# Sample attention of a decode step: its products on VectorE, its loads on GpSimd's queue, key halves on neighbouring partitions

## The chip, the cores and the metric

The kernel runs on one core of one Trainium2 chip. A core has five engines with a queue of instructions each, which run in order: TensorE (PE, with its weight loads shown as PEld), VectorE (DVE), ScalarE (ACT), GpSimd (POOL) and SyncE (SP). Any of SP, ACT and POOL can issue DMA transfers; 16 DMA engines carry them out. Engines wait for each other on semaphores. The metric is the device time of one execution in microseconds.

## The reference

One layer of a hybrid decoder, for a prompt of 1024 tokens and for 8 sequences of 4 new tokens (the sample). Both go through the same projections; the change concerns the attention of the sample's 32 tokens over their cached keys and values. For each of three head groups (window and dilation 128/1, 512/4, 2048/16), with 4 heads of 64 columns:

```python
def _dilated_sample(q, k_all, v_all, slopes, window, dil, L):
    j = jnp.arange(window // dil + 1)
    idx = L + jnp.arange(T)[:, None] - j[None, :] * dil
    valid = idx >= 0
    kg, vg = k_all[:, jnp.maximum(idx, 0)], v_all[:, jnp.maximum(idx, 0)]
    s = jnp.einsum('bthd,btjhd->bhtj', q, kg) * (1.0 / math.sqrt(Dh))
    s = jnp.where(valid, s - slopes * (j * dil), NEG_INF)
    m = jnp.max(s, axis=-1, keepdims=True)
    p = jnp.exp(s - m); l = jnp.sum(p, axis=-1, keepdims=True)
    o = jnp.einsum('bhtj,btjhd->bthd', p / l, vg)
    lse = m + jnp.log(l)
```

The three groups' outputs are combined with weights softmax(lse), projected, gated together with a convolution branch, and added to x; a feed-forward layer, a small per-layer gate and a norm follow. Everything is float32.

## The kernel before, in words

Activations lie transposed, 1056 tokens (1024 of the prompt, 32 of the sample) in three chunks of 352 columns. Each large product is done as three matmuls on float32r parts: a weight slab is loaded by SP (tile wst, L93), ACT rounds it to whi (L103), DVE takes the rest as wlo (L104), and PE runs L120, L121 and L122 into a PSUM tile mm. A tile of eight K-blocks takes 24 matmuls.

The order of stages is: input norm and small projection; convolution projections and gates; then, for two pairs of heads and in each for three groups, the projections q, k, v (copied out of PSUM by ACT at L651), the prompt's scores (L824 on PE into ps_s, and a mask, add and row maximum on DVE, L829), the transposed values (L851), and the sample's tokens, which PE transposes (L859) and SP writes to a small DRAM buffer scr (L862). At the end of a pair comes the prompt's softmax: maxima through PE (L683 to L711), exponentials on ACT (L745), transposes of the scores (L747), copies to pt by ACT (L751) or, for half of the parts of pair 0, DVE (L753), products with the values (L724), and normalisation (L775 to L791). After pair 1 the convolution branch is projected: L886 loads a gate into et (two buffers), 12 matmuls make a tile, DVE multiplies it into et (L891), L892 stores it. Attention output, mixing projection, feed-forward and output follow, without sample attention.

The tiles mm and ps_s have two buffers each in this part, so PE goes on to the tile after next only when the reader of the first has finished.

Sample attention has no matmuls. It is a list of small steps, queued in `bg` by `sample_ops` and taken from there by `pump` between the projections; the Tile scheduler then gives every engine's queue its final order by a simulated timeline. A pair has 2 heads x 32 tokens = 64 rows. The 128 cached keys of a row are cut into two halves of 64: half 0 lies on partitions 0 to 63, half 1 (with the new keys) on partitions 64 to 127. Per pair and group:

- `load` (L546): POOL clears the unused end of the bias tile (L549), SP loads the bias (L552, one DMA for each half) and the query (sq, L555, twice, from scr).
- `k_part`, for eight tiles kt of 8 keys x 64 columns and a tile of new keys: SP loads kt (L584, one DMA for each half, 64 partitions x 2 KB; new keys L595 or L598), POOL multiplies it by the query (L558), DVE sums over the 64 columns (L559).
- `smax`: bias, maximum, exponential (L563 to L566).
- `v_part`, for eight tiles of values and one of new values: POOL multiplies (the first straight into vacc, L571, the others in place, L573) and DVE adds to vacc (L574); at the end DVE sums vacc into oacc (L606).

kt has four buffers, so a load waits until the tile four before it has been summed or added. At the end of a pair `sample_out` combines the groups and the two halves: maxima are exchanged through PE (L612 to L619), and a matmul with `both`, a sum of two identity halves, adds row p and row p + 64 (L630).

Of the kernel before, what the change touches and what calls it, by code (L numbers as in the profile page):

```python
# [13 lines left out]
OP = mybir.AluOpType  # L14
# [15 lines left out]
NEG = -1e30  # L30
DIL = (1, 4, 16)
NB = (8, 8, 8)
SOFF = (0, 132, 261, 390)
# [14 lines left out]
def hybrid_layer(ctx: ExitStack, tc: tile.TileContext, I, O):  # L48
    nc = tc.nc
    te, ve, ac, gp, sy = nc.tensor, nc.vector, nc.scalar, nc.gpsimd, nc.sync  # L50
# [12 lines left out]
    ident = consts.tile([128, 128], F32, name="ident")  # L63
# [240 lines left out]
    scr = [[dram.tile([3, 32, 128], F32, name=f"scr{i}{g}") for g in range(3)] for i in range(2)]  # L304
# [224 lines left out]
    CK, HK = 8, 64  # L529
    oacc = sp.tile([128, 3, 64], F32, name="oacc")  # L530
    sv = sp.tile([128, 8, 3], F32, name="sv")
    vacc = sp.tile([128, CK, 64], F32, name="vacc")
    both = sp.tile([128, 64], F32, name="both")
    ve.tensor_tensor(both, ident[:, :64], ident[:, 64:], op=OP.add)

    def rows(t, width, first, pair, n):

        return bass.AP(tensor=t.tensor, offset=t.offset + 2 * pair * width + first,
                       ap=[[4 * width, 32], [width, 2], [1, n]])

    def sample_ops(pair, g):
        n_new = 4 if g == 0 else 1
        nk = HK + n_new
        st = {}

        def load():  # L546
            st["s"] = sp.tile([128, HK + 4], F32, name="sc", tag="sc", bufs=2)
            st["b"] = b = sp.tile([128, HK + 4], F32, name="sbias", tag="sbias", bufs=2)
            gp.memset(b[0:64, HK:], NEG)  # L549
            for hf in range(2):  # L550
                n = nk if hf else HK
                sy.dma_start(b[64 * hf:64 * hf + 64, :n], rows(I["sbias"], SOFF[3], SOFF[g] + HK * hf, pair, n))  # L552
            st["q"] = a = sp.tile([128, 64], F32, name="sq", tag="sq", bufs=2)
            for hf in range(2):
                sy.dma_start(a[64 * hf:64 * hf + 64], scr[pair][g][0].rearrange("t (e d) -> (t e) d", d=64))  # L555

        def k_part(kt, off, n):
            gp.tensor_tensor(kt, kt, st["q"][:, None, :].to_broadcast([128, n, 64]), op=OP.mult)  # L558
            ve.tensor_reduce(st["s"][:, off:off + n], kt, axis=AX, op=OP.add)  # L559

        def smax():
            s = st["s"][:, :nk]
            ve.tensor_tensor(s, s, st["b"][:, :nk], op=OP.add)  # L563
            ve.tensor_reduce(sv[:, 0, g:g + 1], s, axis=AX, op=OP.max)
            ve.tensor_scalar(sv[:, 1, g:g + 1], sv[:, 0, g:g + 1], -1.0, None, op0=OP.mult)
            ac.activation(s, s, AF.Exp, bias=sv[:, 1, g:g + 1], accum_out=sv[:, 2, g:g + 1])  # L566

        def v_part(vt, off, n):
            p = st["s"][:, off:off + n, None].to_broadcast([128, n, 64])
            if off == 0:  # L570
                gp.tensor_tensor(vacc, vt, p, op=OP.mult)  # L571
            else:
                gp.tensor_tensor(vt, vt, p, op=OP.mult)  # L573
                ve.tensor_tensor(vacc[:, :n], vacc[:, :n], vt, op=OP.add)  # L574

        def kt_tile():
            return sp.tile([128, CK, 64], F32, name="kt", tag="kt", bufs=4)

        def steps(nm, part):
            for i in range(0, HK, CK):  # L580
                def f(i=i):
                    kt = kt_tile()
                    for hf in range(2):
                        sy.dma_start(kt[64 * hf:64 * hf + 64].rearrange("p n d -> p (n d)"),  # L584
                                     rows(I[f"{nm}g{g}"], 128 * 64, (HK * hf + i) * 64, pair, CK * 64))
                    part(kt, i, CK)
                bg.append(f)

            def new():
                kt = kt_tile()  # L590
                src = scr[pair][g]["qkv".index(nm)]
                gp.memset(kt[0:64, :n_new], 0.0)
                if g == 0:
                    for j in range(4):
                        sy.dma_start(kt[64 + 16 * j:80 + 16 * j, :4],  # L595
                                     src.rearrange("(n b) (e d) -> (b e) n d", n=4, d=64))
                else:
                    sy.dma_start(kt[64:, 0], src.rearrange("t (e d) -> (t e) d", d=64))  # L598
                part(kt[:, :n_new], HK, n_new)
            bg.append(new)  # L600

        bg.append(load)
        steps("k", k_part)
        bg.append(smax)
        steps("v", v_part)
        bg.append(lambda: ve.tensor_reduce(oacc[:, g], vacc.rearrange("p n d -> p d n"), axis=AX, op=OP.add))  # L606

    def sample_out(pair):

        ve.tensor_reduce(sv[:, 3, 0:1], sv[:, 0], axis=AX, op=OP.max)  # L610
        ps = misc()
        te.transpose(ps[0:1, :128], sv[:, 3, 0:1], ident)  # L612
        room = sp.tile([128, CK, 64], F32, name="kt", tag="kt", bufs=4)
        row, ow = room[0:1, 0:2], room[:, 2:4].rearrange("p a b -> p (a b)")[:, :65]
        o, so = room[0:64, 4], room[:, 5, :32]
        ve.tensor_copy(row.rearrange("o h t -> o (h t)"), ps[0:1, :128])
        ve.tensor_tensor(row[:, 0], row[:, 0], row[:, 1], op=OP.max)
        ve.tensor_copy(row[:, 1], row[:, 0])
        te.transpose(ps[:, 128:129], row.rearrange("o h t -> o (h t)"), ident[0:1, 0:1])  # L619
        ve.tensor_scalar(sv[:, 3, 1:2], ps[:, 128:129], -1.0, None, op0=OP.mult)  # L620
        ac.activation(sv[:, 4], sv[:, 0], AF.Exp, bias=sv[:, 3, 1:2])
        ve.tensor_tensor(sv[:, 5], sv[:, 4], sv[:, 2], op=OP.mult)
        ve.tensor_reduce(ow[:, 64:65], sv[:, 5], axis=AX, op=OP.add)
        ve.tensor_scalar(ow[:, :64], oacc[:, 0], sv[:, 4, 0:1], None, op0=OP.mult)
        for g in (1, 2):
            ve.scalar_tensor_tensor(ow[:, :64], oacc[:, g], sv[:, 4, g:g + 1], ow[:, :64],
                                    op0=OP.mult, op1=OP.add)

        ps = misc()
        te.matmul(ps[:64, :65], both, ow, start=True, stop=True)  # L630
        ve.reciprocal(sv[:64, 6, 0:1], ps[:64, 64:65])
        ve.tensor_scalar(o, ps[:64, :64], sv[:64, 6, 0:1], None, op0=OP.mult)
        ps = misc()
        te.transpose(ps[:64, :64], o, ident[:64, :64])
        for e in range(2):
            ve.tensor_copy(so[64 * e:64 * e + 64], ps[:64, :64].rearrange("d (t e) -> d e t", e=2)[:, e])
        split(ohi[:, pair, TP:], olo[:, pair, TP:], so)
# [160 lines left out]
    for pair in range(2):  # L798
        S, VT = [], []
        mcol = ap_.tile([128, 3, 8, 2], F32, name="mcol", tag="mcol", bufs=2)  # L800
        for g in range(3):
# [4 lines left out]
            for i, nm in enumerate("qkv"):  # L806
                t = ap_.tile([128, T], F32, name=nm, tag=nm, bufs=1)
# [3 lines left out]
                if i == 1:  # L811

                    q, k = qkv
# [3 lines left out]
                    for b0 in range(0, 8, 2):  # L817

                        pss2 = [pss.tile([128, 2, 256], F32, name="ps_s", tag="ps_s") for e in range(2)]
                        for b in (b0, b0 + 1):  # L820
                            q0, k0, nk, _ = BL[g][b]
                            for e in range(2):
                                h = slice(64 * e, 64 * e + 64)
# [512 lines left out]
```

## Time and profile before

| | |
|---|---|
| time of the runs | 1683.91 us median of 3 (1677.45 to 1688.59) |
| the profiled execution | 1681.99 us, of which 1680.2 us are its span |
| granted TensorE clock in it | 0.988 |
| PE, DVE, ACT, POOL busy | 1619.0, 1038.5, 579.1, 200.0 us |
| DMA | 233.81 MB, mean 139 GB/s |

A page of the profile gives each engine's busy time and, in 40 slices of 42 us, its busy share in tenths. Rows of groups read: line, engine, operation, output <- input, shapes, count | busy us, mean ns of one | idle time of the engine just before, and what ended it. Rows of waits read: engine, line and tile that waited <- what ended the wait: us in total, times, longest. Rows of the timeline read: start, duration, engine, line, operation, with the idle time before it in brackets. "SPq" is the issue of a DMA on SP's queue; busy time of POOL does not contain DMA issues.

### The profile page before, as it was taken

To read this page: it belongs to the slowest core of one execution; us is meant where nothing else is said; L and a number is where in the kernel's file an instruction comes from. 1 tells how busy PE (TensorE), PEld (TensorE's weight loads), DVE (VectorE), ACT (ScalarE), POOL (GpSimd) and SP (SyncE) were. 2 spreads that over 40 slices of the span, in tenths; PEclk is the share of its full clock that TensorE was granted. 3 is DMA by queue.
4 is the path that set the end of the run, shared out by engine and by line. 5 is a ranking of instruction groups with operands and counts; after the bars stand their busy time and mean duration, and the time that the engine had idled before them with its cause. 6 is when DMAs were issued, how large, how long until landed. Compare 5 with 4: busy or idle time off the path is not lost.

```text
span 1680.2 us, 27443 instructions
## 1 busy us (share of the span) xinstructions
PE 1619.0 (96%) x11091; PEld 1584.8 (94%) x11091; DVE 1038.5 (62%) x1791; ACT 579.1 (34%) x1064; POOL 200.0 (12%) x178
## 2 busy tenths in 40 slices
PE   8999999999989988989999999999999999999996
PEld 7999999988889888989999999999999999999996
DVE  7799996125453656475776666676665533437666
ACT  7211223422253325342344333333333321215542
POOL 3100000005550543250000000000000000000003
PEclk9999999999999999999999999999999999999998
DMA  8535554615441457584245444432223422311422
GB/s 306 182 127 177 187 176 151 204 50 158 144 125 34 138 175 221 165 277 160 102 157 200 159 155 161 152 133 77 77 77 118 142 87 85 117 48 57 128 72 108
DMA packets 85487, 233.81 MB, mean 139 GB/s; under 512 B 14576, under 2 KB 32432, under 8 KB 84272
## 3 DMA queue, kind: packets, MB, share of 16 engines
q1 hardware_dynamic: 76272, 174.15, 32.0%
q10 hardware_dynamic: 9088, 57.91, 10.1%
q8 instruction: 87, 1.43, 0.3%
q14 instruction: 40, 0.33, 0.1%
HBM read 187.49 MB, written 88.37 MB: 164 GB/s over the span
## 4 chain that ended last, share of the span: by engine, by line
PE 40%; issue 9%; DVE 7%; DMA 4%; ACT 1%; POOL 0%; SPq 0%; DVEq 0%; ACTq 0%; POOLq 0%
PE mm L203 6%; PE mm L205 6%; PE mm L120 6%; PE mm L204 6%; PE mm L122 6%; PE mm L121 6%; DMA wst<-in_w_fu 2%; DVE wq L145 1%; PE N L724 1%; DVE hlo L209 1%; DVE ws L150 1%; DMA et<-gcd 1%; DVE hq L209 0%; DVE fg L1071 0%; DVE ga L956 0%
## 5 line engine op out<-in xcount | busy, mean ns | idle before, releaser
L120 PE MATMUL mm<-hhi,whi 128*128 128x352 f32 x1424 | 466.7, 328 | 8.4 <-ACT hhi L367 4.4
L121 PE MATMUL mm<-hlo,whi 128*128 128x352 f32 x1424 | 462.7, 325 | 2.0 <-DVE hlo L209 2.0
L122 PE MATMUL mm<-hhi,wlo 128*128 128x352 f32 x1424 | 463.4, 326 | 0.0
L203 PE MATMUL mm<-hq,wq 128*128 128x264 f32 x1232 | 350.7, 285 | 2.3 <-DVE fg L1076 1.9
L204 PE MATMUL mm<-hq,wq 128*128 128x264 f32 x1232 | 350.5, 285 | 2.0 <-DVE hq L209 2.0
L205 PE MATMUL mm<-hq,wq 128*128 128x264 f32 x1232 | 350.3, 285 | 0.0
L120 PEld LDWEIGHTS mm<-hhi,whi 128*128 128x128 f32 x1424 | 269.4, 189 | 14.6 <-ACT hhi L367 4.9
L121 PEld LDWEIGHTS mm<-hlo,whi 128*128 128x128 f32 x1424 | 270.6, 190 | 4.4 <-DVE hlo L209 2.8
L122 PEld LDWEIGHTS mm<-hhi,wlo 128*128 128x128 f32 x1424 | 270.7, 190 | 2.2 <-issue 2.0
L203 PEld LDWEIGHTS mm<-hq,wq 128*128 128x128 f32 x1232 | 232.4, 189 | 3.3 <-ACT fg L1072 2.0
L204 PEld LDWEIGHTS mm<-hq,wq 128*128 128x128 f32 x1232 | 232.6, 189 | 2.4 <-DVE hq L209 2.4
L205 PEld LDWEIGHTS mm<-hq,wq 128*128 128x128 f32 x1232 | 232.1, 189 | 0.0
L103 ACT ACTIVATE whi<-wst 128x1024 fp32r<-128x1024 f32 (+2 forms) x100 | 97.3, 974 | 316.7 <-PE mm L121 303.7
L121 PE MATMUL mm<-mid,whi 128*128 128x352 f32 x528 | 169.5, 323 | 1.6 <-DVE mid L209 1.6
L122 PE MATMUL mm<-mid,wlo 128*128 128x352 f32 x528 | 168.4, 323 | 0.0
L120 PE MATMUL mm<-mid,whi 128*128 128x352 f32 x528 | 167.6, 324 | 0.0
L104 DVE TENSOR_TENSOR wlo<-wst,whi 128x1024 fp32r<-128x1024 f32 (+2 forms) x100 | 115.6, 1157 | 63.5 <-ACT whi L103 62.2
L425 DVE SCALAR_TENSOR_TENSOR acc<-U,vec,acc 128x1024 f32<-128x1024 f32 x120 | 147.1, 1279 | 0.4
L558 POOL TENSOR_TENSOR kt<-kt,sq 128x512 f32<-128x512 f32 (+2 forms) x54 | 68.9, 1300 | 461.4 <-DMA sq<-scr 445.9
L1138 POOL TENSOR_TENSOR y<-x,r 128x704 f32<-128x704 f32 x8 | 15.2, 1944 | 883.4 <-ACT r L938 883.4
L1122 DVE TENSOR_TENSOR x<-mm,x 128x352 f32<-128x352 f32 x96 | 49.4, 523 | 106.5 <-PE mm L122 106.1
L121 PEld LDWEIGHTS mm<-mid,whi 128*128 128x128 f32 x528 | 99.1, 188 | 1.9 <-DVE mid L209 1.9
(214 smaller groups left out, 2129.7 us busy)
## 6 DMA issues: line engine op xcount, KB each, us to landing
o_rest<-in_rest ACTq DMA_DIRECT2D x32, 768.0 KB, 5.3
wst<-in_w_in SPq DMA_DIRECT2D x42, 512.0 KB, 5.3
kt<-in_kg SPq DMA_DIRECT2D x96, 128.0 KB, 2.9
kt<-in_vg SPq DMA_DIRECT2D x96, 128.0 KB, 3.2
midd<-fg ACTq DMA_DIRECT2D x44, 264.0 KB, 3.3
mst<-midd SPq DMA_DIRECT2D x22, 528.0 KB, 4.6
wst<-in_w_fg SPq DMA_DIRECT2D x22, 512.0 KB, 3.9
wst<-in_w_fu SPq DMA_DIRECT2D x22, 512.0 KB, 5.7
```

The source lines that it names most:

```text
L103: last_act[0] = ac.activation(hi[:, :n, :], st[:, :n, :], AF.Copy)
L104: ve.tensor_tensor(lo[:, :n, :], st[:, :n, :], hi[:, :n, :].bitcast(F32), op=OP.subtract)
L120: te.matmul(ps, hi[:, k, :], rh, start=(i == 0), stop=False)
L121: te.matmul(ps, hi[:, k, :], rl, start=False, stop=False)
L122: te.matmul(ps, lo[:, k, :], rh, start=False, stop=(i == n - 1))
L145: ve.tensor_tensor(t[:, 1], x, t[:, 0].bitcast(F32), op=OP.subtract)
L203: te.matmul(ps, w[:, 0, i], h[:, 0, i], start=start and i == 0, stop=False, skip_group_check=True)
L204: te.matmul(ps, w[:, 0, i], h[:, 1, i], start=False, stop=False, skip_group_check=True)
L205: te.matmul(ps, w[:, 1, i], h[:, 0, i], start=False, stop=i == k - 1, skip_group_check=True)
L425: ve.scalar_tensor_tensor(acc[:, ct, :TP], U[:, ct, j:j + TP], vcol(w0 + j), acc[:, ct, :TP], op0=OP.mult, op1=OP.add)
L558: gp.tensor_tensor(kt, kt, st["q"][:, None, :].to_broadcast([128, n, 64]), op=OP.mult)
L1122: ve.tensor_tensor(x1[:, m, cs_(c)], ps[:, :C], x1[:, m, cs_(c)], op=OP.add)
```

## The change

The products of `k_part` and `v_part` are VectorE instructions. Every load of the sample attention is issued from GpSimd's queue. The two halves of a row's keys lie on partitions 2r and 2r + 1 instead of r and r + 64, so that a tile of keys or values is one DMA over 128 partitions (source rows 64 keys apart), and the query one DMA that reads each row twice; bias and new keys go to every second partition. POOL clears the whole bias tile and all rows of the tile of new keys, and the loads then fill the parts that hold data. `both` becomes the sum of the even and the odd columns of the identity, and `sample_out` exchanges maxima between neighbouring columns. Line numbers after the helper are lower by one. The arithmetic is the same.

```diff
-    ve.tensor_tensor(both, ident[:, :64], ident[:, 64:], op=OP.add)
-
-    def rows(t, width, first, pair, n):
-
-        return bass.AP(tensor=t.tensor, offset=t.offset + 2 * pair * width + first,
-                       ap=[[4 * width, 32], [width, 2], [1, n]])
+    ve.tensor_tensor(both, ident[:, 0::2], ident[:, 1::2], op=OP.add)
+
+    def dims(t, offset, ap):
+        return bass.AP(tensor=t.tensor, offset=t.offset + offset, ap=ap)
...
-            gp.memset(b[0:64, HK:], NEG)
+            gp.memset(b, NEG)
             for hf in range(2):
                 n = nk if hf else HK
-                sy.dma_start(b[64 * hf:64 * hf + 64, :n], rows(I["sbias"], SOFF[3], SOFF[g] + HK * hf, pair, n))
+                gp.dma_start(b[hf::2, :n], dims(I["sbias"], 2 * pair * SOFF[3] + SOFF[g] + HK * hf,
+                                                [[4 * SOFF[3], 32], [SOFF[3], 2], [1, n]]))
             st["q"] = a = sp.tile([128, 64], F32, name="sq", tag="sq", bufs=2)
-            for hf in range(2):
-                sy.dma_start(a[64 * hf:64 * hf + 64], scr[pair][g][0].rearrange("t (e d) -> (t e) d", d=64))
+            q = scr[pair][g][0]
+            gp.dma_start(a, dims(q, 0, [[64, 64], [0, 2], [1, 64]]))
 
         def k_part(kt, off, n):
-            gp.tensor_tensor(kt, kt, st["q"][:, None, :].to_broadcast([128, n, 64]), op=OP.mult)
+            ve.tensor_tensor(kt, kt, st["q"][:, None, :].to_broadcast([128, n, 64]), op=OP.mult)
             ve.tensor_reduce(st["s"][:, off:off + n], kt, axis=AX, op=OP.add)
...
             if off == 0:
-                gp.tensor_tensor(vacc, vt, p, op=OP.mult)
+                ve.tensor_tensor(vacc, vt, p, op=OP.mult)
             else:
-                gp.tensor_tensor(vt, vt, p, op=OP.mult)
+                ve.tensor_tensor(vt, vt, p, op=OP.mult)
                 ve.tensor_tensor(vacc[:, :n], vacc[:, :n], vt, op=OP.add)
...
                     kt = kt_tile()
-                    for hf in range(2):
-                        sy.dma_start(kt[64 * hf:64 * hf + 64].rearrange("p n d -> p (n d)"),
-                                     rows(I[f"{nm}g{g}"], 128 * 64, (HK * hf + i) * 64, pair, CK * 64))
+                    gp.dma_start(kt.rearrange("p n d -> p (n d)"),
+                                 dims(I[f"{nm}g{g}"], (2 * pair * 128 + i) * 64,
+                                      [[4 * 128 * 64, 32], [HK * 64, 4], [1, CK * 64]]))
                     part(kt, i, CK)
...
-                gp.memset(kt[0:64, :n_new], 0.0)
+                gp.memset(kt[:, :n_new], 0.0)
                 if g == 0:
                     for j in range(4):
-                        sy.dma_start(kt[64 + 16 * j:80 + 16 * j, :4],
+                        gp.dma_start(kt[32 * j + 1:32 * j + 32:2, :4],
                                      src.rearrange("(n b) (e d) -> (b e) n d", n=4, d=64))
                 else:
-                    sy.dma_start(kt[64:, 0], src.rearrange("t (e d) -> (t e) d", d=64))
+                    gp.dma_start(kt[1::2, 0], src.rearrange("t (e d) -> (t e) d", d=64))
                 part(kt[:, :n_new], HK, n_new)
...
-        row, ow = room[0:1, 0:2], room[:, 2:4].rearrange("p a b -> p (a b)")[:, :65]
+        row, ow = room[0:1, 0:2].rearrange("o a b -> o (a b)").rearrange("o (t h) -> o t h", h=2), room[:, 2:4].rearrange("p a b -> p (a b)")[:, :65]
...
-        ve.tensor_tensor(row[:, 0], row[:, 0], row[:, 1], op=OP.max)
-        ve.tensor_copy(row[:, 1], row[:, 0])
+        ve.tensor_tensor(row[:, :, 0], row[:, :, 0], row[:, :, 1], op=OP.max)
+        ve.tensor_copy(row[:, :, 1], row[:, :, 0])
```

How the change moves instructions on VectorE and on GpSimd's queue stands at the places of the prediction that rest on it, as the build of each kernel lists them: engine queues in order, with the semaphores that an instruction waits for in brackets. DMAHW0 to 7 are transfers issued by SP or ACT, DMASW0 to 7 those issued by POOL; the number 49 is a label of the list.

More of the change, by code (lines that the diff above doesn't have):

```diff
@@ L613, in sample_out @@
         room = sp.tile([128, CK, 64], F32, name="kt", tag="kt", bufs=4)
-        row, ow = room[0:1, 0:2], room[:, 2:4].rearrange("p a b -> p (a b)")[:, :65]
+        row, ow = room[0:1, 0:2].rearrange("o a b -> o (a b)").rearrange("o (t h) -> o t h", h=2), room[:, 2:4].rearrange("p a b -> p (a b)")[:, :65]
         o, so = room[0:64, 4], room[:, 5, :32]
-        ve.tensor_copy(row.rearrange("o h t -> o (h t)"), ps[0:1, :128])
-        ve.tensor_tensor(row[:, 0], row[:, 0], row[:, 1], op=OP.max)
-        ve.tensor_copy(row[:, 1], row[:, 0])
-        te.transpose(ps[:, 128:129], row.rearrange("o h t -> o (h t)"), ident[0:1, 0:1])
+        ve.tensor_copy(row, ps[0:1, :128].rearrange("o (t h) -> o t h", h=2))
+        ve.tensor_tensor(row[:, :, 0], row[:, :, 0], row[:, :, 1], op=OP.max)
+        ve.tensor_copy(row[:, :, 1], row[:, :, 0])
+        te.transpose(ps[:, 128:129], row.rearrange("o t h -> o (t h)"), ident[0:1, 0:1])
         ve.tensor_scalar(sv[:, 3, 1:2], ps[:, 128:129], -1.0, None, op0=OP.mult)
```

## The prediction

> **What bounds the kernel now.** I read the page first, then the stage of the sample attention by windows, then who waited for whom in it, last the stretch around one wait.
>
> ```profile
> span 1680.2 us, 27443 instructions
> PE 1619.0 (96%) x11091; PEld 1584.8 (94%) x11091; DVE 1038.5 (62%) x1791; ACT 579.1 (34%) x1064; POOL 200.0 (12%) x178
> PE   8999999999989988989999999999999999999996
> DVE  7799996125453656475776666676665533437666
> POOL 3100000005550543250000000000000000000003
> ```
>
> PE is busy for 96% of the span, so a change elsewhere can only remove or add PE's gaps. POOL works between about 370 and 700 us, on the lines of this change, and there PE's digits fall to 8 in a few slices. The same stretch in us (columns: PE, PEld, DVE, ACT, POOL busy, granted clock, DMA):
>
> ```profile
> 360.00:410.00 50.00, 47.04 (x281) 42.99 (x281) 24.36 (x52) 13.24 (x22) 23.26 (x21) 1.00 0.41 123
> ...
> sum 400.00, PE 371.11 PEld 344.35 DVE 221.16 ACT 144.46 POOL 163.47; mean PE 46.39 PEld 43.04 DVE 27.65 ACT 18.06 POOL 20.43
> ```
>
> From 360 to 760 us PE is idle for 400 - 371 = 29 us: all that a perfect change here could give, 1.7% of the span. DVE is busy for 221 of the 400. Who keeps PE waiting, and what DVE and POOL wait for (us in total, times, longest):
>
> ```profile
> PE ps_s L824 <- DVE mcol L829: 13.0, 12, 2.4
> PE N L724 <- DVE pt L753: 3.5, 1, 3.5
> PE mm L120 <- DVE et L891: 3.4, 2, 2.1
> PE ps_s L747 <- DVE pt L753: 1.3, 1, 1.3
> ...
> DVE sc L559 <- POOL kt L558: 60.8, 34, 12.1
> DVE vacc L574 <- POOL kt L573: 31.9, 18, 3.8
> ...
> POOL kt L573 <- DMA kt<-in_vg: 20.8, 11, 4.9
> POOL kt L558 <- DMA kt<-in_kg: 13.3, 10, 2.9
> ```
>
> PE waits for DVE: 13.0 us for the masks of the prompt's scores (L829), 4.8 us for the copies of transposed scores (L753), 3.4 us for the conv projection's evacuation (L891). DVE in turn sat 60.8 + 31.9 = 92.7 us waiting for POOL's products, and POOL for the loads of keys and values. One stretch shows the chain:
>
> ```profile
> 396.95 4.58 SPq L584 DMA_DIRECT2D kt<-in_vg  x5
> 401.63 1.94 SPq L595 DMA_DIRECT2D kt<-scr  x4
> ...
> 403.25 4.51 POOL L573 TENSOR_TENSOR kt<-kt,sc 128x512 f32<-128x512 f32 x4 [2.69 <-DMA kt<-in_vg]
> ...
> 404.33 2.96 DVE L574 TENSOR_TENSOR vacc<-vacc,kt 128x512 f32<-128x512 f32 x2 [3.02 <-POOL kt L573]
> 407.22 0.28 DVE L829 CUSTOM_DVE_ANT_0 S<-ps_s,bias 128x128 f32<-128x128 f32 x1
> ...
> 402.64 0.32 PE L120 MATMUL mm<-hhi,whi 128*128 128x352 f32 x1
> 402.80 0.32 PE L121 MATMUL mm<-hlo,whi 128*128 128x352 f32 x1
> 407.90 0.92 PE L824 MATMUL ps_s<-k,q 64*128 64x128 f32 x4 [2.21 <-DVE mcol L829]
> ```
>
> Two adds on DVE wait 3.02 us for POOL, POOL 2.69 us for a load on SP's queue; the mask behind them comes at 407.22 and PE loses 2.21 us. Matmuls start 0.16 us apart, so a tile of 24 covers 3.9 us of such lateness, and a tile of 12 in the conv projection 1.9 us.
>
> **The change part by part.** (1) The products of L558, L571 and L573 go from POOL to DVE. Group 0 of pair 0, value half, on DVE, before (L574 the add, L829 a mask):
>
> ```order
> L829 ISA S_3507,mcol<-ps_s,bias 128x256
> L829 ISA mcol 128x1
> L574 TENSOR_TENSOR vacc<-vacc,kt 128x512 [waits DMAHW0_49,DMAHW6_49,DVE_49,Pool_49]
> L574 TENSOR_TENSOR vacc<-vacc,kt 128x512 [waits DMAHW1_49,DMAHW2_49,DVE_49,Pool_49]
> L829 ISA S_3507,mcol<-ps_s,bias 128x128 [waits PE_49]
> ```
>
> and now, one line number lower (L572 is the product, L573 the add):
>
> ```order
> L828 ISA S_3498,mcol<-ps_s,bias 128x256
> L828 ISA mcol 128x1
> L573 TENSOR_TENSOR vacc<-vacc,kt 128x512 [waits DVE_49]
> L572 TENSOR_TENSOR kt<-kt,sc 128x512 [waits DMASW7_49]
> L573 TENSOR_TENSOR vacc<-vacc,kt 128x512 [waits DVE_49]
> L572 TENSOR_TENSOR kt<-kt,sc 128x512 [waits DMASW0_49]
> L573 TENSOR_TENSOR vacc<-vacc,kt 128x512 [waits DVE_49] x2
> L828 ISA S_3498,mcol<-ps_s,bias 128x128 [waits PE_49]
> ```
>
> Between the same two masks stand now four adds and two products instead of two adds, and DVE itself waits for POOL's loads (DMASW), with the mask and, further on, the weight splits of L104 queued behind. The prices:
>
> ```profile
> L574 DVE TENSOR_TENSOR vacc<-vacc,kt 128x512 f32<-128x512 f32 x42 | 41.8, 995 | 32.9 <-POOL kt L573 31.9
> L559 DVE TENSOR_REDUCE sc<-kt 128x8 f32<-128x512 f32 x48 | 32.7, 684 | 60.8 <-POOL kt L558 60.8
> L104 DVE TENSOR_TENSOR wlo<-wst,whi 128x1024 fp32r<-128x1024 f32 x22 | 30.9, 1405 | 2.1 <-ACT whi L103 1.9
> ...
> L145 DVE TENSOR_TENSOR wq<-ws,wq 128x512 fp32r<-128x512 f32 x76 | 52.1, 685 | 3.6 <-ACT wq L144 3.6
> ...
> L104 DVE TENSOR_TENSOR wlo<-wst,whi 128x1024 fp32r<-128x1024 f32 x21 | 25.7, 1224 | 45.0 <-ACT whi L103 45.0
> ...
> L574 DVE TENSOR_TENSOR vacc<-vacc,kt x48: 216/693/1576, 393.8 to 690.5; 128x512 f32<-128x512 f32 x42, 128x64 f32<-128x64 f32 x4, 128x256 f32<-128x256 f32 x2
> ```
>
> The L145 and the last L104 row are from stretches where POOL is idle (900 to 1300 and 100 to 340 us). So a two-input operation of 512 columns costs DVE 0.69 us alone and 0.995 us on average beside POOL, 1.58 at worst. Added: 96 full products x 0.69 = 66 us, 12 short ones at between 0.22 and 0.69, taken as 0.3, 4 us: 70. Given back with POOL out of the way: 42 adds x (0.995 - 0.69) = 13, 22 splits x (1.405 - 1.224) = 4. DVE's work rises by 53, from 221 to 274 of 400 us, and the 92.7 us of waits for POOL go. Per tile of values DVE took 0.995 + 31.9/48 = 1.66 us, of keys 0.684 + 60.8/54 = 1.81; now 1.38 and whatever it waits for the load.
>
> (2) The loads leave SP's queue. POOL's queue at the same place, before:
>
> ```order
> L571 TENSOR_TENSOR vacc<-kt,sc 128x512 [waits DMAHW3_49,DMAHW4_49,PE_49,Activation_49]
> L573 TENSOR_TENSOR kt<-kt,sc 128x512 [waits DMAHW6_49,DMAHW5_49]
> L573 TENSOR_TENSOR kt<-kt,sc 128x512 [waits DMAHW7_49,DMAHW0_49,Pool_49]
> L573 TENSOR_TENSOR kt<-kt,sc 128x512 [waits DMAHW2_49,DMAHW1_49,Pool_49]
> L573 TENSOR_TENSOR kt<-kt,sc 128x512 [waits DMAHW4_49,DMAHW3_49,Pool_49]
> ```
>
> and now (L594 loads the new keys or values of group 0, L582 a tile, L550 the bias):
>
> ```order
> L591 MEMSET kt 128x256 [waits DMASW1_49,DVE_49]
> L594 DMA kt<-scr_123 16x4x64 [waits Pool_49]
> L594 DMA kt<-scr_123 16x4x64 [waits DMASW6_49]
> L594 DMA kt<-scr_123 16x4x64 [waits DMASW7_49]
> L594 DMA kt<-scr_123 16x4x64 [waits DMASW0_49]
> L582 DMA kt<-in_vg 128x1x512 [waits DMASW2_49,DVE_49]
> L582 DMA kt<-in_vg 128x1x512 [waits DMASW3_49,DVE_49]
> ```
>
> POOL now only issues: 96 tile loads (one per tile instead of two), 12 of biases, 6 of queries, 24 of new rows: 138, 23 per pair and group. The value loads stand behind the four of L594. The trace has no DMA issued from POOL; its nearest rows:
>
> ```profile
> L584 SPq DMA_DIRECT2D kt<-in_kg x96: 528/582/1059, 53.5 to 658.6; - x96
> L558 POOL TENSOR_TENSOR kt<-kt,sq x54: 315/1292/2280, 376.3 to 663.4; 128x512 f32<-128x512 f32 x48, 128x64 f32<-128x64 f32 x4, 128x256 f32<-128x256 f32 x2
> DMA to landing us min/median/max: 1.6/2.9/6.2
> ...
> 444.42 1.04 POOL L573 TENSOR_TENSOR kt<-kt,sc 128x512 f32<-128x512 f32 x1
> ...
> sq<-scr SPq DMA_DIRECT2D x12, 16.0 KB, 2.0
> scr<-stok SPq DMA_DIRECT2D x6, 48.0 KB, 2.1
> ```
>
> Lower bound of one issue: SP's median, 0.58 us. Upper: POOL's slowest instruction over 128 rows, held up by DVE, 2.28. I take 1.04, POOL undisturbed over 128 rows, because it too must visit 128 rows. A freed buffer is needed again three tiles later, 3 x 1.38 = 4.1 us, against 1.04 + 2.9 = 3.9 us for issue and landing: barely no wait, except where four reduces or the four L594 come first. Taken as 1 us for each of 6 key halves and 3 us for each of 4 halves of group 0: 18 us of DVE idle, far under the 92.7. At 0.58 it is less than half of that; at 2.28 POOL's queue is slower than DVE (2.28 against 1.38 per tile), the third rival. By the Trainium skill, DMA: Bandwidth & Descriptors, section Specifications, the first byte comes at about 1 us from gpsimd against 0.6 from sync or scalar; 0.4 us more would turn the barely hidden load into a wait of 0.2 us per tile. No run here shows it.
>
> (3) What reaches PE. Masks: per three tiles ahead of a mask DVE is 3 x 0.28 = 0.84 us sooner, if the load is there; over 12 waits 10 us at most, of which I take half, since the four adds and two products above are more between two masks than before: -5 us. SP's queue loses about 200 of its issues, so the loads of L886 behind them come sooner: PE waits at most 3.4 us there, I take -2. Against it, the conv projection, where a tile covers only 1.9 us. DVE before (L891 the evacuation):
>
> ```order
> L104 TENSOR_TENSOR wlo<-wst,whi 128x1024 [waits Activation_49]
> L574 TENSOR_TENSOR vacc<-vacc,kt 128x512 [waits DMAHW2_49,DMAHW1_49,Pool_49]
> L891 TENSOR_TENSOR et<-mm,et 128x352 [waits DMAHW1_49,DMAHW2_49,DVE_49,PE_49]
> L574 TENSOR_TENSOR vacc<-vacc,kt 128x512 [waits DMAHW4_49,DMAHW5_49,DVE_49,Pool_49]
> ```
>
> and now:
>
> ```order
> L890 TENSOR_TENSOR et<-mm,et 128x352 [waits DMAHW4_49,DMAHW5_49,DVE_49,PE_49]
> L570 TENSOR_TENSOR vacc<-kt,sc 128x512 [waits DMASW1_49,Activation_49]
> L572 TENSOR_TENSOR kt<-kt,sc 128x512 [waits DMASW2_49]
> L572 TENSOR_TENSOR kt<-kt,sc 128x512 [waits DMASW3_49]
> L572 TENSOR_TENSOR kt<-kt,sc 128x512 [waits DMASW4_49]
> L890 TENSOR_TENSOR et<-mm,et 128x352 [waits PE_49]
> ```
>
> Four products, 2.8 us, stand between two evacuations that PE wants 1.9 us apart: 0.9 us late, at some five such places, +4 us, more if a load is late. The copies of L752 get a product ahead of them (0.69 us) at three or four places of pair 0 where PE already waited: +2. Layout on neighbouring partitions and the other identity sum change no instruction's size: 0, hidden under PE.
>
> The sum on the profiled execution, 1682.0 us (span 1680.2 and 1.8 around it): 1682 - 5 - 2 + 4 + 2 = 1681. That execution lies 1.9 us under the median of 1683.9, so I forecast 1683, no change that a measurement of this kernel can tell (about 1%).
>
> **The rivals.** Their times are on the profiled execution's scale; the median's lies 2 us higher. First, faster: the masks' waits were wholly POOL's and SP's fault, and DVE's idle half swallows the products. 13.0 + 4.8 + 3.4 = 21.2 us of PE's waits vanish: 1682 - 21 = 1661. For it speaks the chain at 404 us; against it, that products now stand ahead of the same masks. Second, DVE becomes the bound where its slack is short: late loads add to the four products, and each of the 24 evacuations of the conv projection is 0.9 us late (22 us): 1704 less the SP gain, 1702. The order above speaks for it; the idle 126 us left on DVE (400 - 274) against. Third, slower: POOL's issues limit. A group and pair takes about 50 us (the windows); 23 issues and 4.1 us for the query's way through memory (2.1 + 2.0) exceed that from 2.0 us per issue. At 2.28 the stage is 23 x 2.28 + 4.1 = 56.5 us, 6 us over, six times: 1682 + 36 = 1718. POOL's instructions held up to 2.28 us by DVE speak for it, the undisturbed 1.04 against. By the Trainium skill, SBUF — State Buffer, section "SBUF: two separate sides", DVE keeps GpSimd from writing descriptors in its two-port mode, while two SBUF inputs collide only with a GpSimd operation that reads SBUF; the moved products are of the second kind, so by that rule the third rival would not come about and the sum above stands.
>
> **How the numbers follow.** Forecast 0.66, first rival 0.14, second 0.10, third 0.10. The forecast's own range is 1669 to 1698: all of PE's waits for masks and 2 us at L886 gone and nothing lost (1683.9 - 15), or the losses of (3) doubled and 0.75 us more before each of the 12 masks that PE waited for (1683 + 6 + 9). To leave out no more than 2 in 10 the range takes in most of the first rival and the second, not the third: 1660 to 1708. Faster by over 1% (below 1667) holds the first rival alone, 0.13; slower (above 1701) the third and most of the second, 0.19; within, 0.68.
>
> **What would show it.** Right: POOL without tensor work from 370 to 700 us, DVE near 274 + 18 us of work and load waits in the stage, the adds at 0.69 us and L104 at 1.22; PE's wait for masks between 5 and 12 us, for L890 above 3.4. Wrong: DVE waiting over 60 us for loads of kt (third rival), PE's idle time in the stage under 12 us (first), or adds still near 1 us, which would say that POOL's descriptor work collides with DVE as its products did.

## The result and the profile after

The changed kernel takes 1665.14 us (median of 7 runs, 1664.24 to 1673.99) against 1682.88 us before (median of 7, 1677.45 to 1688.59): a ratio of 0.991, 95% interval 0.9881 to 0.9938. Faster by about 1%, where I had forecast 1683 us. The seven runs of the changed kernel lie in two groups, four at 1664 to 1665 us and three at 1672 to 1674; the profiled execution (1672.1 us) is of the upper one, so its trace shows 10 of the 18 us.

Busy times of the page after, and the stage from 360 to 760 us by windows (columns as in the prediction):

```profile
span 1670.3 us, 27130 instructions
PE 1616.8 (97%) x11091; PEld 1583.6 (95%) x11091; DVE 1074.6 (64%) x1899; ACT 579.1 (35%) x1064; POOL 142.8 (9%) x208
```

```profile
360.00:410.00 50.00, 50.00 (x302) 45.57 (x301) 31.47 (x76) 15.55 (x26) 14.62 (x29) 1.00 0.40 126
410.00:460.00 50.00, 50.00 (x323) 46.92 (x322) 32.02 (x87) 14.56 (x29) 12.35 (x25) 1.00 0.53 174
...
550.00:600.00 50.00, 50.00 (x300) 45.24 (x299) 36.82 (x89) 13.64 (x25) 17.87 (x36) 1.00 0.52 165
...
sum 400.00, PE 379.10 PEld 352.65 DVE 262.64 ACT 147.71 POOL 102.56; mean PE 47.39 PEld 44.08 DVE 32.83 ACT 18.46 POOL 12.82
```

PE is idle for 21 instead of 29 us of the 400. POOL's busy time does contain its DMA issues, other than said ahead: of its 102.6 us in these windows 71 are issues (L582, L594, L550, L597, L554), and besides these it does nothing before 700 us but 3 us of clearing. What PE waited for in the stage, and DVE:

```profile
PE mm L120 <- DVE et L890: 3.7, 3, 1.4
PE N L723 <- DVE bcot L790: 2.9, 2, 2.0
PE ps_s L823 <- DVE mcol L828: 2.6, 2, 2.3
PE N L723 <- ACT pt L750: 1.9, 1, 1.9
...
PE ps_s L746 <- DVE pt L752: 0.8, 1, 0.8
```

```profile
DVE kt L557 <- DMA sq<-scr: 25.0, 5, 7.7
...
DVE kt L572 <- DMA kt<-in_vg: 11.9, 8, 3.4
...
DVE kt L557 <- DMA kt<-in_kg: 6.8, 11, 1.5
```

The masks' wait fell from 13.0 to 2.6 us. DVE no longer stands for GpSimd's products (92.7 us) but for loads: 25.0 us for the query (sq), 21.3 for keys and values (the two rows, and 2.6 for new keys). The prices, by groups in the stage:

```profile
L557 DVE TENSOR_TENSOR kt<-kt,sq 128x512 f32<-128x512 f32 x48 | 31.4, 685 | 32.0 <-DMA sq<-scr 25.0 <-DMA kt<-in_kg 6.8
...
L573 DVE TENSOR_TENSOR vacc<-vacc,kt 128x512 f32<-128x512 f32 x42 | 28.8, 686 | 0.2
L104 DVE TENSOR_TENSOR wlo<-wst,whi 128x1024 fp32r<-128x1024 f32 x23 | 28.4, 1233 | 8.7 <-ACT whi L103 8.7
```

```profile
L582 POOL DMA_DIRECT2D kt<-in_vg x48 | 26.3, 549 | 71.9 <-DVE vacc L573 28.8 <-DVE vacc L570 24.4 <-DVE sc L558 8.7
```

The products take 0.685 us, the adds 0.686 instead of 0.995, the splits 1.233 instead of 1.405; an issue on POOL's queue 0.55 us. The one long mask wait that is left is the predicted chain, one engine shorter. From the chain that ended last, the load (start, us); then DVE's and PE's timelines behind it:

```profile
601.65 6.98 DMA kt<-in_vg
```

```profile
608.66 0.69 DVE L572 TENSOR_TENSOR kt<-kt,sc 128x512 f32<-128x512 f32 x1 [3.40 <-DMA kt<-in_vg]
609.27 0.69 DVE L573 TENSOR_TENSOR vacc<-vacc,kt 128x512 f32<-128x512 f32 x1
609.87 0.29 DVE L828 CUSTOM_DVE_ANT_0 S<-ps_s,bias 128x128 f32<-128x128 f32 x1
```

```profile
610.43 1.13 PE L823 MATMUL ps_s<-k,q 64*128 64x128 f32 x8 [2.34 <-DVE mcol L828]
```

A load of values takes 6.98 us where the median is 3.5, the product waits 3.40 us for it, the mask stands behind, and PE loses 2.34 us. While it was on its way the DMA engines were nearly all busy (last but one column of a window of 1 us, their share):

```profile
604.00:605.00 1.00, 1.00 (x8) 1.00 1.03 361
```

### The profile page after: what moved, and what is told of

The parts are those of the page before. It is cut to its first block, busy times and chain, and to the rows that moved or that the text cites. A ratio compares the mean times of both kernels' runs of the same rounds, so it can differ in the third digit from the quotient of the medians.

```text
span 1670.3 us, 27130 instructions
## 1 busy us (share of the span) xinstructions
PE 1616.8 (97%) x11091; PEld 1583.6 (95%) x11091; DVE 1074.6 (64%) x1899; ACT 579.1 (35%) x1064; POOL 142.8 (9%) x208
## 4 chain that ended last, share of the span: by engine, by line
PE 72%; issue 13%; DVE 7%; DMA 4%; ACT 2%; POOL 1%; SPq 0%; DVEq 0%; POOLq 0%; ACTq 0%
PE mm L120 15%; PE mm L122 15%; PE mm L121 15%; PE mm L203 7%; PE mm L205 7%; PE mm L204 7%; PE ps_s L823 1%; PE N L723 1%; DMA wst<-in_w_fu 1%; ACT S L744 1%; DVE hlo L209 1%; DMA kt<-in_vg 1%; DVE wq L145 1%; PE ps_s L746 1%; DVE ws L150 0%
## 5 line engine op out<-in xcount | busy, mean ns | idle before, releaser
L104 DVE TENSOR_TENSOR wlo<-wst,whi 128x1024 fp32r<-128x1024 f32 (+2 forms) x100 | 111.8, 1119 | 69.4 <-ACT whi L103 68.1
L121 PEld LDWEIGHTS mm<-mid,whi 128*128 128x128 f32 x528 | 99.1, 188 | 1.9 <-DVE mid L209 1.9
L122 PEld LDWEIGHTS mm<-mid,wlo 128*128 128x128 f32 x528 | 98.8, 188 | 0.0
L120 PEld LDWEIGHTS mm<-mid,whi 128*128 128x128 f32 x528 | 98.6, 188 | 0.2 <-ACT mid L208 0.2
```

Of the source, the lines that this page charges most:

```text
L104: ve.tensor_tensor(lo[:, :n, :], st[:, :n, :], hi[:, :n, :].bitcast(F32), op=OP.subtract)
L120: te.matmul(ps, hi[:, k, :], rh, start=(i == 0), stop=False)
L121: te.matmul(ps, hi[:, k, :], rl, start=False, stop=False)
L122: te.matmul(ps, lo[:, k, :], rh, start=False, stop=(i == n - 1))
```

## The experiments

The change has three parts: products to DVE, loads to POOL's queue, and the layout that makes one transfer of a tile instead of two. Each is a few lines, so the runs apply them singly and in pairs; others place the halves differently or only add work. All ratios are to the kernel before, with 95% intervals; the last three columns are from the profiled executions, 360 to 790 us: PE's idle time, its wait for masks, and the time that DVE stood for the sample's loads or for POOL's products. PE's idle time alone does not rank the kernels: TensorE's clock also falls at times (last section), which cost e5 15.4 us of this stage and e2 27.3, against 6.8 before; and the profiled execution of e5 is the slowest of its eleven (1680.15 us, median 1675.62).

| kernel | products | loads | per tile | ratio | PE idle | masks | DVE stood |
|---|---|---|---|---|---|---|---|
| before | POOL | SP | 2 | 1 | 29.2 | 13.0 | 92.7 |
| e1_products | DVE | SP | 2 | 1.0014 (0.9996 to 1.0031) | 27.4 | 5.3 | 57.8 |
| e2_queue | POOL | POOL | 2 | 1.0098 (1.0072 to 1.0124) | 50.4 | 0 | 31.7 |
| e5_layout | POOL | SP | 1 | 0.9948 (0.9931 to 0.9965) | 19.6 | 7.1 | 78.5 |
| e3_sp_loads | DVE | SP | 1 | 0.9884 (0.9862 to 0.9907) | 15.5 | 0.3 | 42.1 |
| e4_two_loads | DVE | POOL | 2 | 0.9843 (0.9821 to 0.9866) | 10.5 | 0.3 | 19.0 |
| after | DVE | POOL | 1 | 0.991 (0.9881 to 0.9938) | 20.9 | 2.6 | 46.3 |
| e14_queue_layout | POOL | POOL | 1 | 0.9812 (0.9788 to 0.9836) | 9.7 | 0.3 | 55.4 |
| e9_sp_two | DVE | SP | 2, new rows | 0.9915 (0.9891 to 0.9938) | 18.2 | 0.3 | 52.4 |
| e10_gpsimd_two | DVE | POOL | 2, new rows | 0.9839 (0.9814 to 0.9863) | 9.4 | 0.3 | 16.2 |
| e8_more_vectore | after + 34 us of DVE | | | 0.9875 (0.9853 to 0.9897) | 15.2 | 0.3 | 30.7 |
| e11_clear_tiles | after + 49 us of POOL | | | 0.985 (0.9832 to 0.9869) | 13.3 | 0.3 | 31.6 |
| e13_products_more | e1 + 34 us of DVE | | | 0.9952 (0.9936 to 0.9968) | 23.5 | 2.5 | 47.6 |
| e12_products_clear | e1 + 48 us of POOL | | | 0.9963 (0.9946 to 0.998) | 23.6 | 6.5 | 55.8 |

"New rows" means neighbouring partitions, as in the change, but a transfer for each half.

**First: which part?** My theory A was the first rival's: DVE no longer waits for POOL's products ahead of masks, so the products are the gain. Against it stood B (SP's queue) and C (one transfer).

Products alone:

```diff
-            gp.tensor_tensor(kt, kt, st["q"][:, None, :].to_broadcast([128, n, 64]), op=OP.mult)
+            ve.tensor_tensor(kt, kt, st["q"][:, None, :].to_broadcast([128, n, 64]), op=OP.mult)
...
-                gp.tensor_tensor(vt, vt, p, op=OP.mult)
+                ve.tensor_tensor(vt, vt, p, op=OP.mult)
```

> Only the products move to VectorE; loads stay on SP, two for each tile, halves on partitions 0-63 and 64-127. Theory A (the gain is VectorE no longer waiting 92.7 us for products on GpSimd ahead of masks): PE's wait for masks falls from 13.0 us to 5 or less, adds near 0.69 us, and the time to about 1670 (ratio 0.990 to 0.995). Theory B (the gain is that some 200 issues leave SP's queue, so that what stands behind them comes sooner): masks and time stay within 3 us of before (0.998 to 1.003). Theory C (the gain is one transfer for each tile instead of two): as B. My prediction's own sum would have it a little slower, by the products that stand ahead of evacuations: +1 us.

Measured 1.0014: theory A falls, though its own mark is nearly there (5.3 us, 5 or less expected). PE's waits in the stage, and DVE's:

```profile
PE mm L120 <- DVE et L891: 8.4, 4, 3.9
PE ps_s L824 <- DVE mcol L829: 5.3, 4, 1.9
```

```profile
DVE kt L558 <- DMA sq<-scr: 27.5, 5, 7.8
...
DVE kt L573 <- DMA kt<-in_vg: 17.3, 20, 3.1
```

The masks gained 7.7 us, the conv projection lost 5.0 (L891: 3.4 before): the loss that the prediction had put at 4, in the kernel that has only this part. PE's idle time fell by 1.8 us in all, and stretches of lower clock (last section) took 5.1 us more in the stage than before. The stall did not go, it moved: DVE now stands 57.8 us for loads.

Queue alone, in `sample_ops` of the kernel before:

```diff
-                    for hf in range(2):
-                        sy.dma_start(kt[64 * hf:64 * hf + 64].rearrange("p n d -> p (n d)"),
+                    for hf in range(2):
+                        gp.dma_start(kt[64 * hf:64 * hf + 64].rearrange("p n d -> p (n d)"),
```

(and the bias, query and new rows in the same way).

> Only the queue changes: GpSimd issues the loads (two for each tile) and still makes the products. Theory A: no gain, PE's wait for masks 13 us or more; GpSimd has some 250 issues of 0.55 us = 137 us on top of 163 us of tensor work, so products come later: ratio 1.000 to 1.006. Theory B: SP's queue is free, ratio 0.990 to 0.995. Theory C: no gain, 1.000.

Measured 1.0098: slower, as theory A had it, but beyond its 1.006 and without its mark, since PE never waits for a mask. The stage in three windows (us, PE busy, matmuls, clock) and the waits of the last one:

```profile
360.00:600.00 240.00, 236.16 (x1581) 1.00 0.37 112
600.00:700.00 100.00, 93.13 (x697) 0.97 0.65 209
700.00:790.00 90.00, 50.34 (x261) 0.73 0.67 200
```

```profile
PE misc L619 <- DVE kt L618: 19.4, 1, 19.4
PE mm L120 <- DVE ga L956: 9.2, 7, 2.0
PE misc L612 <- DVE sv L610: 6.3, 1, 6.3
```

Until 700 us PE is idle for 10.7 us (before: 22.9): the queue alone more than halves the waits that were to be removed. But POOL, with products and 240 issues, is late with the last group (its last load of a tile leaves at 747 us, at 683 before), and PE stands for `sample_out`: 19.4 us at L619, 6.3 at L612 and 3.0 at L630 of the 39.7 that it is idle from 700 to 790, against 6.3 in all before. So B was right on the stage and A on the end.

The change with its loads back on SP, one transfer for each tile:

```diff
-                    gp.dma_start(kt.rearrange("p n d -> p (n d)"),
+                    sy.dma_start(kt.rearrange("p n d -> p (n d)"),
```

> The changed kernel with its loads back on SP, one for each tile, products on VectorE, halves on neighbouring partitions. Theory A: as the changed kernel, ratio 0.988 to 0.994, VectorE's waits for loads about the same 46 us. Theory B: the gain goes, 0.998 to 1.002. Theory C: as A.

0.9884: the gain does not need POOL's queue.

Products and queue, without the layout (the kernel before with the first two edits together):

> Products on VectorE and loads on GpSimd, but two transfers of 64 partitions for each tile and the old partitions of the halves. GpSimd issues 46 instead of 23 transfers for each pair and group, 25 us at 0.55 us of about 50. Theory A: as the changed kernel, 0.988 to 0.994. Theory B: the same. Theory C: the gain goes, 0.997 or more. The rival of the prediction in which GpSimd's issues limit: 46 x 0.55 is half of the time that a group has, so no loss from that; if VectorE's waits for loads double to 90 us, it was near.

0.9843, better than the whole change: C falls as the sole cause. 46 issues for each pair and group do not limit, and DVE's waits for loads did not double but fell to 19.0 us.

**Second: layout alone, and added work.** These runs took theory D (products and timely loads are both needed) against E (fewer issues are a gain by themselves), and theory F: what decides is the order in which the scheduler puts DVE's instructions, which every edit shifts. Layout alone, that is, the change with two of its edits taken back everywhere:

```diff
-            ve.tensor_tensor(kt, kt, st["q"][:, None, :].to_broadcast([128, n, 64]), op=OP.mult)
+            gp.tensor_tensor(kt, kt, st["q"][:, None, :].to_broadcast([128, n, 64]), op=OP.mult)
...
-                    gp.dma_start(kt.rearrange("p n d -> p (n d)"),
+                    sy.dma_start(kt.rearrange("p n d -> p (n d)"),
```

> Only the layout changes: halves on neighbouring partitions, one load of 128 partitions for each tile, loads on SP, products on GpSimd. Theory D (the gain needs both the products on VectorE and loads that come in time, with fewer issues on SP or none): no gain alone, VectorE still waits some 90 us for GpSimd's products, ratio 0.997 to 1.003. Theory E (fewer issues on SP are a gain by themselves, and the products only add to it): 0.993 to 0.996, with GpSimd's 34 us of waits for loads falling by half.

0.9948, E's number: D falls. POOL's waits for cached keys and values are 20.8 us against 34, but those for new rows rose from 0.4 to 11.4, so the sum hardly fell (32.2 against 34.5 us), and E's mark, half of 34, is missed. These two rows carry the 20.8:

```profile
POOL kt L572 <- DMA kt<-in_vg: 13.2, 10, 3.5
POOL kt L557 <- DMA kt<-in_kg: 7.6, 7, 2.5
```

The changed kernel with each sum of keys made twice:

```diff
             ve.tensor_reduce(st["s"][:, off:off + n], kt, axis=AX, op=OP.add)
+            ve.tensor_reduce(st["s"][:, off:off + n], kt, axis=AX, op=OP.add)
```

> The changed kernel with every sum of a tile of keys made twice (48 x 0.68 us + small ones = 34 us more VectorE work in the stage, the second sum overwriting the first with the same). It prices the products that stand ahead of masks and evacuations. Theory D (VectorE's lateness decides, and most of it is standing still for loads, so that work put there fills standing time): 0 to +6 us on the changed kernel, 0.991 to 0.995 of before. If VectorE is already the bound where its slack is short (the second rival of the prediction): +15 us or more, 1.000 or more.

0.9875, below both numbers expected, its interval overlapping that of the changed kernel: with 34 us more on DVE the kernel is no slower. DVE's amount of work is not the limit; what the 34 us cost by themselves is not separated from the shift of the order.

Two transfers for each tile on neighbouring partitions, on SP and on POOL:

```diff
-                    gp.dma_start(kt.rearrange("p n d -> p (n d)"),
-                                 dims(I[f"{nm}g{g}"], (2 * pair * 128 + i) * 64,
-                                      [[4 * 128 * 64, 32], [HK * 64, 4], [1, CK * 64]]))
+                    for hf in range(2):
+                        gp.dma_start(kt[hf::2].rearrange("p n d -> p (n d)"),
+                                     dims(I[f"{nm}g{g}"], (2 * pair * 128 + HK * hf + i) * 64,
+                                          [[4 * 128 * 64, 32], [128 * 64, 2], [1, CK * 64]]))
```

> Products on VectorE, halves on neighbouring partitions, loads on SP, but two transfers of 64 partitions (even, odd) for each tile: as the kernel with loads back on SP (0.988), with the number of issues doubled. If the number of SP's issues is what took the gain away from the products alone (1.001): 0.997 to 1.003, VectorE's waits for loads near 57 us. If it was where the halves lie: 0.986 to 0.991, waits near 40.

> The changed kernel with two transfers of 64 partitions (even, odd) for each tile instead of one: strictly more for GpSimd to issue. Theory F (the extra gain of the kernel with two loads, 0.984, comes from the order: the scheduler counts more time for two loads and so places the products farther back on VectorE, where the loads have landed): 0.982 to 0.987, VectorE's waits for sq at most 10 us against 25, although more is issued. If it was where the halves lie: as the changed kernel, 0.988 to 0.994.

On POOL 0.9839, as F said and as e4 (0.9843): where the halves lie changes nothing there, and more issues are faster by 0.7%. On SP 0.9915, at the edge of the lower range expected, but with waits (52.4 us) nearer to those of the other, so that run does not decide between them. It differs from the products alone (1.0014) only in where the halves lie, with one transfer for the query and POOL's clears that go with it: on SP that is worth 1.0 point, on POOL nothing, and why is open. In the change and in the kernel with two transfers on POOL, the start of the second group's key products on DVE:

```
after:            L828 ISA S_3498,mcol<-ps_s,bias 128x256
                  L828 ISA mcol 128x1
                  L557 TENSOR_TENSOR kt<-kt,sq 128x512 x4
two transfers:    L606 TENSOR_REDUCE oacc<-vacc 128x64
                  L104 TENSOR_TENSOR wlo<-wst,whi 128x1024
                  L557 TENSOR_TENSOR kt<-kt,sq 128x512 x3
```

In after they stand directly behind masks, ahead of the weight split (L104); with two transfers behind that split. What DVE waited for there, all groups:

```profile
DVE wlo L104 <- ACT whi L103: 24.4, 12, 5.4
DVE S L829 <- PE ps_s L824: 21.8, 18, 3.6
...
DVE kt L557 <- DMA sq<-scr: 7.6, 1, 7.6
```

7.6 us against 25.0, and DVE now waits mainly for PE and ACT, that is, it is ahead.

To shift the order without touching the transfers, the change with one more instruction on POOL ahead of each load:

```diff
+                    gp.memset(kt[:, :8], 0.0)
                     gp.dma_start(kt.rearrange("p n d -> p (n d)"),
```

> The changed kernel, its loads as they are (one transfer for each tile), but GpSimd first clears the whole tile, which the load then overwrites: strictly more work, and every load leaves later. In the build, the first product of four of the six groups now stands behind the last sum of the group before. Theory F (the order that the scheduler gives VectorE decides, and a dearer load pushes the products back to where their data have landed): VectorE's waits for sq fall below 15 us from 25, and the time to 0.983 to 0.988 although there is more to do. If the shorter transfers were the gain of the kernels with two loads: 0.990 to 0.997, as the changed kernel or worse.

0.985: with 92 clears of 0.545 us, and each load later by as much, the kernel is faster than the change (the intervals do not meet). The query's wait is 10.8 us; two further waits of that product, 8.2 us together, have no releaser in the profile, so the mark is less clear than the time. The same two additions on the kernel with the products alone, the second sums and the clear (`gp.memset(kt, 0.0)` ahead of its two loads):

> Products on VectorE, loads on SP in two transfers, old partitions (the kernel whose time stayed at 1.001), with every sum of keys made twice: 34 us more VectorE work. In the build the four products that stood between two evacuations of the conv projection stand now one or two at a time. Theory F (order): PE's wait for L891 falls from 8.4 us to 4 or less and the time to 0.990 to 0.996 although there is more to do. If the old partitions or SP's issues cost the gain: 1.001 to 1.010, as before or slower by the extra work.

> Products on VectorE, loads on SP in two transfers, old partitions (1.001), and GpSimd clears each tile before its loads, which overwrite it: no work for VectorE added, every load later. In the build the four products between two evacuations of the conv projection are three, a softmax maximum ahead of one sum, and the products of the fifth group stand behind the last sum of the fourth. Theory F (order): 0.988 to 0.997, though loads are later. If two issues for each tile on SP with the old partitions take the gain away: 1.000 to 1.008.

0.9952 and 0.9963: both faster than the products alone (1.0014), though both only add work. L892, the evacuation, waits 6.2 us in the first (4 or less was expected) and 2.0 in the second.

**Third: the change without its products.**

```diff
-            ve.tensor_tensor(kt, kt, st["q"][:, None, :].to_broadcast([128, n, 64]), op=OP.mult)
+            gp.tensor_tensor(kt, kt, st["q"][:, None, :].to_broadcast([128, n, 64]), op=OP.mult)
...
```

(all three products back on POOL, loads and layout as changed.)

> The change without its first part: loads on GpSimd's queue, one for each tile, halves on neighbouring partitions, products still on GpSimd. GpSimd has some 140 issues of 0.55 us = 77 us beside 163 us of products, against 250 issues and 1.010 in the kernel with the queue alone. If products on VectorE are needed for the gain: 0.998 to 1.008. If freeing SP and halving the transfers are a gain by themselves: 0.985 to 0.995.

0.9812 (1653.67 us median): the fastest of all kernels here, beyond both ranges expected. The stage in three windows, POOL's key products, and DVE's waits:

```profile
360.00:600.00 240.00, 237.73 (x1603) 0.99 0.39 127
600.00:700.00 100.00, 95.96 (x712) 0.98 0.69 228
700.00:790.00 90.00, 86.60 (x527) 1.00 0.55 186
```

```profile
L557 POOL TENSOR_TENSOR kt<-kt,sq 128x512 f32<-128x512 f32 x48 | 62.2, 1312 | 14.3 <-DMA kt<-in_kg 10.9 <-DMA sq<-scr 3.2
```

```profile
DVE sc L558 <- POOL kt L557: 34.8, 21, 9.0
DVE S L828 <- PE ps_s L823: 29.9, 17, 2.9
DVE vacc L573 <- POOL kt L572: 20.6, 13, 2.9
```

The products still take 1.31 us on POOL, DVE still stands 55.4 us for them, and PE is idle for 9.7 us. DVE's standing time is thus no measure of the loss. The wait for the query (25.0 us of DVE in the changed kernel) is here POOL's own, 3.2 us in the row of L557. The loads stand less too: for a buffer that DVE's sums or adds still held, tile loads waited 114.1 us on POOL's queue in the changed kernel, 21.6 in this one; on SP's queue before, they stood 45.0 us for DVE's sums, adds and masks.

So, shown: the layout with the queue, without the products, gives 1.9%, and the products on top take 1.0 points of it back (0.9812 to 0.991, intervals apart), while on SP they add 0.6 (0.9948 to 0.9884). Both of the first two are more than pure extra work moved these kernels (0.4 to 0.7 points faster, the smallest within the intervals; on SP doubling the issues, e3 to e9, gave 0.3 slower, also within them), the third is not. But the size of the second hangs on the order too: against the kernel with products on DVE and two transfers (0.9839) only 0.3 points remain, within the intervals. The parts do not add up: the order shifts with each, and the queue alone gives POOL 240 issues beside the products, with the layout 138, so that the last load of a tile leaves at 668 us and not at 747.

Argued, not shown: that it is the place of the query's wait in the order that costs the changed kernel its point; no kernel here changes that place and nothing else. The trace speaks against a direct cost: these waits end at 377, 422, 463, 589 and 634 us, and from 360 to 460 and from 550 to 600 us PE is not idle at all (first section). The changed kernel loses its time later. From 600 to 700 us, where e14 is idle for 4.0 us, it is idle for 10.8, at a lower clock:

```profile
600.00:700.00 100.00, 89.21 (x612) 0.95 0.61 203
```

```profile
PE mm L120 <- DVE et L890: 3.7, 3, 1.4
PE ps_s L823 <- DVE mcol L828: 2.3, 1, 2.3
```

Whether the query's wait that ends at 589 us delays the loads up to the mask at 610 us was not tested. Nor was a kernel with more than four buffers for kt, though the loads wait for these. Open is also what keeps the products alone at 1.001, when both kernels that only add work to them are faster.

## Why the prediction was right or wrong, point by point

- **The range and the forecast.** 1665.14 us lies in 1660 to 1708, but that range had been widened to take in the first rival; the forecast's own, 1669 to 1698, misses it, and a time below 1667 had been given 0.13. So the range held by luck: by the room left for a rival whose mechanism did not come, and not by the sum.
- **The bound.** "All that a perfect change here could give" was 29 us of PE's idle time. Wrong: the last experiment gave 30.1 us of span with 9.7 us still idle. Of these, 19.5 are idle time and 3.4 the clock's stretches (below), which I had not counted; 7 are not placed.
- **(1) Products.** Right in every price: 0.685 us for the products where 0.69 was taken, the adds' relief 42 x (0.995 - 0.686) = 13.0 us, the splits' 22 x (1.405 - 1.233) = 3.8. DVE is busy for 263 instead of 274 us of the window, in part because instructions in a row overlap: four products at 376.86 us take 2.50 us and not 4 x 0.685 = 2.74. That the amount of work is not what costs is what the 34 us added say, though they shift the order too.
- **(2) Loads.** The issue costs 0.55 us, a little under the lower bound of 0.58; I had taken 1.04, because an issue too must visit 128 rows, but over 64 rows it takes as long (median 0.54 us in e10, 0.54 over 128 rows in the changed kernel); so the third rival was never near. Landing went from 2.9 to 3.5 us. DVE's waits for loads are 46.3 us, not 18: keys and values 21.3, near the estimate, but 25.0 for the query, which my sum left out and named only in the third rival. By the Trainium skill, DMA: Bandwidth & Descriptors, section Specifications, the first byte comes at about 1 us from gpsimd and at 0.6 from sync. From issue to landing the runs do not settle it: one-transfer loads land in 3.5 us from POOL and in 3.4 to 3.5 from SP (e3), the query in 2.0 and 2.1; without the products, in 3.5 to 3.8 from POOL (e14) and 3.1 to 3.3 from SP (e5), the query in 2.0 from both.

```profile
kt<-in_kg POOLq DMA_DIRECT2D x48, 256.0 KB, 3.5
...
sq<-scr POOLq DMA_DIRECT2D x6, 32.0 KB, 2.0
```

```profile
kt<-in_kg SPq DMA_DIRECT2D x48, 256.0 KB, 3.5
kt<-in_vg SPq DMA_DIRECT2D x48, 256.0 KB, 3.4
sq<-scr SPq DMA_DIRECT2D x6, 32.0 KB, 2.1
```

- **(3) What reaches PE.** This is the step that failed: it put the loads' place in the queues at almost nothing and let the products' place cost as much as it won. Masks: -5 was taken as half of 10, -10.4 came; the half was taken because more products stand between two masks, and PE's waits there show no cost of these. The sign of being right, 5 to 12 us of mask waits, was missed at 2.6. Conv projection: +4 was taken, +0.3 came at L890 (3.4 to 3.7); a loss of that size came only in the kernel with the products alone (+5.0) and in one that adds to it (+2.8). Copies: +2 was taken; the waits for L752 fell from 4.8 to 0.8, with 2.3 more for L790 and 1.6 more for ACT's copies. The -2 for the issues that SP's queue loses was one of the two smallest terms and should have been the largest: in the runs, layout and queue together, without the products, are 30 us (e14).
- **The sum.** -1 us on the profiled scale, -10 measured: PE's idle time from 360 to 790 us fell by 8.3 us (29.2 to 20.9), the clock's stretches there took 3.4 us more, and 5 us of the span's 9.9 I have not placed. On the median the gap is 18 us, since the profiled execution is of the upper group of its runs.
- **The rivals.** The first (21.2 us of PE's waits vanish, 1663 on the median's scale) is nearest to the median, but not by its mechanism: its mark, PE idle under 12 us, is missed by the changed kernel and met by e4, e10 and e14. The second (conv projection) shows only in e1 and, smaller, in e13. The third fell with the price of an issue. The rule of the Trainium skill that I had weighed there, SBUF — State Buffer, section "SBUF: two separate sides", agrees with the trace: beside DVE's products an issue on POOL took 0.52 to 0.56 us in the mean of each line, in e14, without them, 0.53 to 0.58.

## What to carry to other kernels

When an engine's product is late, look first at where its data stand in a queue: here the kernel with its products untouched, and slow, was 1.9% faster once their loads had another queue and half the transfers (and, with these, another order). A wait moved from a helper engine to the one that also serves the bottleneck is put in front of everything behind it, so price it by what that queue then delays and not by its length: 25.0 us of waits for the query passed without PE idle beside most of them. Where a scheduler orders the queues, test an edit against one that adds harmless work: a difference smaller than what that gives (here up to 0.7%) cannot be put down to the edit.

## What the runs showed of the hardware that was not expected

TensorE's clock falls in stretches of about 3.4 us at half speed. The changed kernel in windows of 1 us (us, PE busy, matmuls, clock):

```profile
481.00:482.00 1.00, 1.00 (x9) 0.91 0.93 229
482.00:483.00 1.00, 1.00 (x6) 0.50 0.52 136
483.00:484.00 1.00, 1.00 (x5) 0.50 0.95 377
484.00:485.00 1.00, 1.00 (x5) 0.50 0.75 246
485.00:486.00 1.00, 1.00 (x7) 0.88 0.16 61
```

Each costs some 1.7 us, and a window of 10 us then shows 0.83. Summed over such windows from 360 to 790 us the loss is 6.8 us before, 10.2 after, 11.9 with the products alone, 3.4 in e14. The Trainium skill, TensorE: Matmul & The Clock Gate, section "What's actually happening", has such windows of about 3.4 us at half clock behind idle ones. The length agrees, and most stretches do follow a gap, though mostly a shorter one: in the 6 us ahead of each of the four before, PE was idle for 1.8 to 2.9 us, ahead of five of the six after for 0.9 to 2.3. So a wait of PE can cost 1.7 us on top of itself: the mask's 2.34 us that end at 610.43 are followed by a stretch from 611 to 615. But ahead of the one shown, and of both in e14, PE was not idle at all, and its longest wait from 470 to 500 us was 0.8 us; what starts these is open. And beside POOL's products a DVE add took 0.995 us (before) and 1.04 us (e14) against 0.686 without them, and e14, where this costs DVE 15 us (42 x 0.35), is still the fastest kernel.
